# A two-layer decoder trunk on one core: order of the first contraction, place of the gates' projection, a lookup that yields, and products grouped by shape

## The chip, the cores and the metric

The kernel runs on one core of a Trainium2 chip. The metric is the device time of one execution in microseconds (us), the median of several. PE is TensorE (matmuls), DVE VectorE, ACT ScalarE, POOL GpSimd, SP the engine whose queue issues most transfers.

## What is computed

512 tokens of width 1024 go through two layers. Each layer has a mixer and a PEER channel mixer (product-key experts), each followed by a layer norm of alpha * h + sublayer(h). Cut to what matters here:

```python
def mixer_ab(x, w_in, pool_w, pool_scale, ret_norm_g, w_out):      # layer 0
    u, q, k, v, g = jnp.split(x @ w_in, AB_SPLITS, axis=-1)
    y_a = pool_mixer(u, pool_w, pool_scale)       # causal means over 2/4/8/16, then a product per group
    q, k = rotary(q), rotary(k) * 64 ** -0.5
    o = retention(q, k, v)                        # 4 heads, chunks of 128
    y_b = head_layernorm(o, ret_norm_g) * silu(g)
    return concat([y_a, y_b]) @ w_out

def hgrn2_chunkwise(q, k, v, logf):               # layer 1: 8 heads, chunks of 32
    b = cumsum(logf)                              # within a chunk
    q_in, k_in, k_out = q * exp(b), k * exp(-b), k * exp(b_last - b)
    ...

def peer(x, w_q, sub_keys, u_tab, v_tab):
    q = (x @ w_q).reshape(T, 8, 2, 128)
    s_top, i_top = top_k(einsum(q, sub_keys), 16)          # over 128 keys, per head and half
    best, pos = top_k(all sums of two halves' s_top, 16)
    eid, gate = cand_id[pos], softmax(best)                # an expert is a pair of keys
    act = gelu(einsum(x, u_tab[eid]))
    return einsum(gate * act, v_tab[eid])

h = layer_norm(alpha * h + mix);  h = layer_norm(alpha * h + peer(h))
```

All matrices are float32; u_tab and v_tab have 16384 rows of 1024.

## The kernel before

**Products.** A float32 operand is split into two fp32r parts, hi and lo: `split` lets ACT cast hi and DVE subtract to get lo (L76, L77). `mm3` then makes three matmuls per 128 rows of contraction, hi*hi, lo*hi and hi*lo (L92 to L94). `stream` loads a weight tile into `raw` over SP's queue (L82) and splits it. Nearly all weights and all experts pass this way, so ACT and DVE work for each of PE's blocks. PSUM has three pools: psA (2 tiles, pA), psB (3, pB), psC (3, pC).

**Order.** The tile scheduler keeps the order in which the program names operations on each engine as far as priorities and buffers let it. Generators (`look`, `rounds`) interleave two programs by hand: `route_topk` and `route_gates` yield a cost, and for every 2.8 of credit `lookahead` issues one block of experts (128 experts: 24 matmuls of 128x384 into one PSUM tile, then GELU into `ge`).

**Start** (`run`). The identity is loaded first, then four pairs of 256 rows of x (transposed, `xT`) and of the first weight; the pool projection then goes output by output, each over the whole contraction.

**Layer 0's mixer** (`mixer_ab`). In this order: pool projection with its sums and the product with pool_w (`pool_part`; its output times pool_scale is `ya`), gates' projection (silu into `sgs`), queries and keys with rotation, values, retention (`kn`, `sc`, `state`), normalization of the heads, output projection. `ya` is split into the output projection's operand after retention.

**Layer 1's mixer** (`mixer_c`, `decays`). For each head and each of four blocks of 128 tokens three kinds of products go to one pC tile: 128x128 (L463), two of 32x32 (L465) and one of 64x64 (L468).

**PEER** (`peer`). A layer norm per block of tokens (`tb`) writes `xT`; alpha is then multiplied into `hs` (L597). Three of the four blocks of tokens (384) go through all experts densely: `route_topk` finds keys, `lookup` turns positions into key numbers ka and kb by comparing and summing over 16 candidates on DVE (L794 to L803), PE transposes ka, kb and gate into pC (L730), and `route_gates` builds one-hot matrices `oh` (L758, against the iota `iot` of L744) and `og` (L759) and multiplies them into a dense gate matrix (L765, L766), stored as `gd`. The fourth block (tb = 3) gathers its experts' rows by indirect transfers instead. Meanwhile `lookahead` computes the first NLA groups of 4 blocks; all but the last KEEP of them are spilled to DRAM (`sp`) and come back later. `experts` then loads `gt` from `gd`, multiplies `ge` by it (L884), splits into ch and cl and accumulates the product with v_tab (L914) into six PSUM tiles, while the remaining blocks are computed.

## Time and profile before

| | us |
|---|---|
| median of three runs | 2922.81 (2922.74 to 2922.95) |
| profiled execution | 2923.92 |
| its span, first to last instruction | 2922.1 |
| PE busy | 2880.0 |
| DVE busy | 2388.3 |
| ACT busy | 1170.4 |

A busy share is a mean over stages. The stages in order of the profiled execution: layer 0's mixer to about 170 us, its routing with blocks ahead to 545, its experts to about 1410; layer 1's mixer to about 1680, routing to 2053, experts to the end.

### The profile page before, as it was taken

The page shows a single profiled execution, that of the slowest core. Times are in us where ns is not written, and L with a number is a line of the kernel's source. Part 1 is how long each engine was busy: PE and PEld are TensorE (multiplying, and loading weights), DVE is VectorE, ACT ScalarE, POOL GpSimd, SP SyncE. Part 2 cuts the span into 40 slices and gives each one's busy share as a digit, 9 for nine tenths or more (in the row PEclk, how much of TensorE's full clock was granted, in tenths as well). Part 3 has the DMA queues.
Part 4 walks back from the last instruction along what each step waited for, and adds up shares of the span by engine and source line. Part 5 has one row for each costly group of instructions (what it writes and reads, how often), then busy time and mean ns, then how long its engine had stood idle before and what let it go on. Part 6 is the DMA issues. An engine that isn't in the chain of part 4 may idle for free.

```text
span 2922.1 us, 42467 instructions
## 1 busy us (share of the span) xinstructions
PE 2880.0 (99%) x15822; PEld 2564.3 (88%) x15822; DVE 2388.3 (82%) x4500; ACT 1170.4 (40%) x1730; POOL 697.1 (24%) x538
## 2 busy tenths in 40 slices
PE   8999999999999999999999999999999999999998
PEld 6788999988888888888888889999988898898897
DVE  5679999788888888886687689999788888888875
ACT  3233555433333333334433433655433333333333
POOL 0000000144444444440000000000344444444420
PEclk9999999999999999999999999999999999999999
DMA  6232469999999989994322233489999999999972
GB/s 219 80 105 98 134 207 296 317 372 337 351 329 347 355 332 339 359 337 161 99 80 69 87 102 113 145 255 291 361 346 336 353 339 340 351 345 336 359 283 69
DMA packets 282927, 740.26 MB, mean 253 GB/s; under 512 B 21600, under 2 KB 120416, under 8 KB 282720
## 3 DMA queue, kind: packets, MB, share of 16 engines
q1 hardware_dynamic: 208992, 469.08, 46.3%
q0 software_dynamic: 73728, 268.47, 24.7%
q8 instruction: 124, 2.03, 0.3%
q14 instruction: 83, 0.68, 0.1%
HBM read 667.73 MB, written 69.73 MB: 252 GB/s over the span
## 4 chain that ended last, share of the span: by engine, by line
PE 87%; DVE 10%; issue 1%; ACT 1%; DMA 1%; POOL 0%; SPq 0%; ACTq 0%; POOLq 0%; DVEq 0%
PE pC L914 18%; PE pB L914 18%; PE pA L92 15%; PE pA L93 15%; PE pA L94 15%; PE pB L765 2%; DVE lo L77 1%; PE pB L766 1%; DVE s L677 1%; DVE ix L679 1%; DVE ix L676 1%; DVE stop L675 0%; DVE xp L795 0%; DVE xp L794 0%; DVE oh L758 0%
## 5 line engine op out<-in xcount | busy, mean ns | idle before, releaser
L77 DVE TENSOR_TENSOR lo<-raw,hi 128x1024 fp32r<-128x1024 f32 x608 | 739.9, 1219 | 190.3 <-ACT hi L76 186.5
L92 PE MATMUL pA<-xThi,hi 128*128 128x384 f32 (+2 forms) x2496 | 861.9, 345 | 12.0 <-ACT hi L76 8.7
L76 ACT CAST hi<-raw 128x1024 fp32r<-128x1024 f32 x608 | 638.3, 1052 | 587.8 <-PE pA L93 480.2
L93 PE MATMUL pA<-xTlo,hi 128*128 128x384 f32 (+2 forms) x2496 | 858.8, 344 | 0.7 <-DVE xTlo L155 0.7
L94 PE MATMUL pA<-xThi,lo 128*128 128x384 f32 (+2 forms) x2496 | 858.3, 344 | 0.0
L814 POOL DMA_INDIRECT row<-in_u,eid x256 | 390.6, 1526 | 942.4 <-DVE av L824 628.9
L92 PEld LDWEIGHTS pA<-xThi,hi 128*128 128x128 f32 x2496 | 470.3, 188 | 34.6 <-ACT hi L76 9.2
L93 PEld LDWEIGHTS pA<-xTlo,hi 128*128 128x128 f32 x2496 | 470.4, 188 | 21.8 <-DVE xTlo L155 0.9
L94 PEld LDWEIGHTS pA<-xThi,lo 128*128 128x128 f32 x2496 | 470.2, 188 | 16.2 <-DVE lo L77 0.9
L76 ACT CAST ch<-ge 128x384 fp32r<-128x384 f32 x256 | 131.7, 515 | 626.0 <-PE pC L914 493.1
L814 POOL DMA_INDIRECT row<-in_v,eid x256 | 300.1, 1172 | 179.4 <-DVE h L833 111.7
L833 DVE SCALAR_TENSOR_TENSOR h<-row,cf,h 128x1024 f32<-128x1024 f32 x256 | 328.5, 1283 | 0.0
L824 DVE CUSTOM_DVE_ANT_0 row<-row,x 128x1024 f32<-128x1024 f32 x256 | 311.5, 1218 | 0.0
L914 PE MATMUL pC<-hi,ch 128*128 128x512 f32 x768 | 300.8, 392 | 0.0
L914 PE MATMUL pB<-lo,ch 128*128 128x512 f32 x768 | 300.5, 391 | 0.0
L914 PE MATMUL pC<-hi,cl 128*128 128x512 f32 x768 | 300.0, 391 | 0.0
L914 PE MATMUL pB<-hi,cl 128*128 128x512 f32 x768 | 299.3, 390 | 0.0
L914 PE MATMUL pB<-hi,ch 128*128 128x512 f32 x768 | 298.9, 389 | 0.0
L914 PE MATMUL pC<-lo,ch 128*128 128x512 f32 x768 | 298.5, 389 | 0.0
L77 DVE TENSOR_TENSOR cl<-ge,ch 128x384 fp32r<-128x384 f32 x256 | 142.6, 557 | 178.6 <-ACT ch L76 175.5
L914 PEld LDWEIGHTS pC<-lo,ch 128*128 128x128 f32 x768 | 144.2, 188 | 32.0
L914 PEld LDWEIGHTS pB<-hi,cl 128*128 128x128 f32 x768 | 144.1, 188 | 31.8
(252 smaller groups left out, 3432.9 us busy)
## 6 DMA issues: line engine op xcount, KB each, us to landing
raw<-in_peer_ut SPq DMA_DIRECT2D x256, 512.0 KB
raw<-in_peer_v SPq DMA_DIRECT2D x256, 512.0 KB
gd<-gbuf SPq DMA_DIRECT2D x24, 2048.0 KB
gt<-gd SPq DMA_DIRECT2D x64, 768.0 KB
sp<-ge SPq DMA_DIRECT2D x22, 768.0 KB
ge<-sp SPq DMA_DIRECT2D x22, 768.0 KB
raw<-in_peer_w_q SPq DMA_DIRECT2D x32, 512.0 KB
raw<-in_c_w_in SPq DMA_DIRECT2D x32, 512.0 KB
```

The source lines that it names most:

```text
L76: self.nc.scalar.copy(hi, src)
L77: return self.nc.vector.tensor_tensor(lo, src, hi.bitcast(F32), ALU.subtract)
L92: nc.tensor.matmul(ps, ah, bh, start=(i == 0), stop=False)
L93: nc.tensor.matmul(ps, ah, bl, start=False, stop=False)
L94: nc.tensor.matmul(ps, al, bh, start=False, stop=(i == n - 1))
L676: nc.vector.max_index(out=ix[:, 0:8], in_max=mx[:, 0:8], in_values=sc)
L677: nc.vector.match_replace(out=s2, in_to_replace=mx[:, 0:8], in_values=sc, imm_value=NEG)
L765: nc.tensor.matmul(pg[:, sl], oh[:, 0, a, :, b], og[:, 0, a, :, b], start=True, stop=False)
L814: nc.gpsimd.indirect_dma_start(out=t, out_offset=None, in_=io[name], in_offset=bass.IndirectOffsetOnAxis(ap=self.eid[:, j:j + 1], axis=0))
L824: nc.vector.tensor_tensor_reduce(ur, ur, x3, 1.0, 0.0, ALU.mult, ALU.add, av[:, k:k + 1])
L833: nc.vector.scalar_tensor_tensor(acc, vr, coefs[i // GQ][:, i % GQ:i % GQ + 1], acc, ALU.mult, ALU.add)
L914: nc.tensor.matmul(acc[hf], a[:, ts], b[:, hf * 512:(hf + 1) * 512], start=first and i == 0, stop=last and i == 2)
```

## The change

- `run`: 14 matmuls on a zeroed tile are issued first (`warm`); x and the first weight come in chunks as before, but the first pair in two halves each; the identity is loaded after them.
- `proj_T` with `early="k"`: the pool projection goes over four quarters of the contraction outermost, with the four outputs in two pA and two pB tiles; `mm3` gets `first` and `last` for that.
- `mixer_ab`: the pooling sums follow the queries and keys' projection; the gates' projection follows retention, with the splits of `ya` and the transposes of the heads inside its sink; they write the old `xT`.
- `decays`: the three kinds of products are issued kind by kind for the four blocks of tokens.
- `peer`: alpha is applied to `hs` only for tb = 3 (on ACT), and for the others in the addition at the end of `experts`; the iota is made before routing.
- `lookup` yields between its steps; every second block of the look-ahead uses a pC tile; NLA is 14 instead of 13; the yield of a gate step is 1.4 instead of 1.2.

```diff
-NLA = 13
+NLA = 14
-ALT = False
-Y2 = 1.2
+Y2 = 1.4
-    def mm3(self, ps, pairs):
+    def mm3(self, ps, pairs, first=True, last=True):
...
+        if early == "k":
+            pss = [self.psA.tile([P, 512], F32, name="pA", tag="pA") for _ in range(2)] + \
+                  [self.psB.tile([P, 512], F32, name="pB", tag="pB") for _ in range(2)]
+            ops = [pairs(i, slice(0, T)) for i in range(4)]
+            for a, b in ((0, 2), (2, 4), (4, 6), (6, 8)):
+                for i in range(4):
+                    self.mm3(pss[i], ops[i][a:b], a == 0, b == NDC)
+                    if b == NDC:
+                        sink(j * 4 + i, pss[i])
+            return
...
             self.proj_T(w, 1, xT, sink_qk)
+            for n in range(4):
+                sums(n)
...
-            yT = self.new_xT()
-            for n in range(4):
-                self.split(ya[n], yT[0][:, n, :], yT[1][:, n, :])
...
+            def sink_g(j, tb, ps):
+                sg = ab.tile([P, 512], F32, name="sg%d" % tb, tag="sg%d" % tb)
+                nc.scalar.activation(sg, ps, AF.Sigmoid)
+                nc.vector.tensor_tensor(sg, sg, ps, ALU.mult)
+                nc.vector.tensor_tensor(sg, sg, ng, ALU.mult)
                 ov = o[:, tb].rearrange("p h e -> p (h e)")
-                nc.vector.tensor_tensor(ov, ov, sgs[tb], ALU.mult)
-                self.transpose_in(ov, yT, 4, 4, tb)
-        return yT
+                nc.vector.tensor_tensor(ov, ov, sg, ALU.mult)
+                if tb % 2:
+                    c = slice((tb - 1) * P, (tb + 1) * P)
+                    for n in range(4):
+                        self.split(ya[n][:, c], xT[0][:, n, c], xT[1][:, n, c])
+                if tb:
+                    turn(tb - 1)
+
+            self.proj_N(w, 3, xT, sink_g)
+            turn(NTB - 1)
+        return xT
...
                 for tb in range(NTB):
-                    t0 = tb * P
-                    ts = slice(t0, t0 + P)
+                    ts = slice(tb * P, (tb + 1) * P)
                     nc.tensor.matmul(pc[:, ts], k[:, ts], q[h][:, ts], start=True, stop=True)
+                for t0 in range(0, T, P):
                     for c in (0, 2):
                         nc.tensor.matmul(pc[32 * c:32 * c + 32, t0 + 32 * c + 32:t0 + 32 * c + 64],
...
+                for tb in range(NTB):
+                    t0 = tb * P
                     nc.tensor.matmul(pc[0:64, t0 + 64:t0 + 128], kh[:, tb].rearrange("p c s -> p (c s)"),
...
-                nc.vector.tensor_scalar(hs[tb], hs[tb], ALPHA, None, ALU.mult)
+                    nc.scalar.mul(hs[tb], hs[tb], ALPHA)
...
-                self.mm1(layer, g * NB + b, xT, ge[:, b, :], ALT and (g * NB + b) % 3 == 2)
+                self.mm1(layer, g * NB + b, xT, ge[:, b, :], b % 2 == 1)
...
-                kk = self.lookup(rs2, pos, i0, i1, thr, i16)
-                yield 9.0
+                kk = yield from self.lookup(rs2, pos, i0, i1, thr, i16)
...
             nc.vector.tensor_tensor(x, x, cst[:, None, None, :].broadcast_to(sx), op)
+            yield 2.0
             nc.vector.tensor_tensor(x, x, val[:, :, None, :].broadcast_to(sx), ALU.mult)
+            yield 2.0
...
-                    nc.vector.tensor_tensor(z, z, accs[tb][hf], ALU.add)
+                    nc.vector.scalar_tensor_tensor(z, z, ALPHA, accs[tb][hf], ALU.mult, ALU.add)
...
+    def warm(self):
+        nc = self.nc
+        with self.tc.tile_pool(name="wm", bufs=1) as wm:
+            z = wm.tile([P, 512], F16, name="z", tag="z")
+            nc.gpsimd.memset(z, 0.0)
+            ps = self.psC.tile([P, 512], F32, name="pC", tag="pC")
+            for _ in range(14):
+                nc.tensor.matmul(ps, z[:, :P], z, start=True, stop=True)
...
+            if k == 0:
+                wr = self.raw.tile([P, 2, T], F32, name="raw", tag="raw")
...
+                for a in range(2):
+                    nc.sync.dma_start(out=raw[:, a], in_=io["xT"][:, a, :])
+                    nc.sync.dma_start(out=wr[:, a], in_=wsrc[:, a])
+                for a in range(2):
+                    self.split(raw[:, a], xT[0][:, a, :], xT[1][:, a, :])
+                    self.split(wr[:, a], hi[:, a], lo[:, a])
```

Where the instructions stand. The new lines have other numbers: L76 and L77 become L75 and L76, L279 becomes L280, L295 L296, L463/L465/L468 L484/L487/L492, L758 and L759 L781 and L782, L884 L911.

DVE in layer 0's retention, between the decayed keys kn and the scores sc, before (`lo<-raw,hi` is the split of a weight tile, `xTlo<-ya` that of the pooling output):

```order
L279 TENSOR_TENSOR kn_762<-pC,kdec 128x512
L279 TENSOR_TENSOR kn_763<-pC,kdec 128x512
L77 TENSOR_TENSOR xTlo<-ya_188,xThi 128x512
L77 TENSOR_TENSOR xTlo<-ya_230,xThi 128x512
L77 TENSOR_TENSOR xTlo<-ya_275,xThi 128x512
L77 TENSOR_TENSOR xTlo<-ya_323,xThi 128x512
L77 TENSOR_TENSOR lo<-raw,hi 128x1024
L295 TENSOR_TENSOR sc_812<-pB,dmask 128x512
```

and now, from the last of the pool's outputs on:

```order
L391 TENSOR_SCALAR ya_514<-pB,psc 128x512
L76 TENSOR_TENSOR lo<-raw,hi 128x1024 x3
L280 TENSOR_TENSOR kn_649<-pC,kdec 128x512
L280 TENSOR_TENSOR kn_650<-pC,kdec 128x512
L76 TENSOR_TENSOR lo<-raw,hi 128x1024
L296 TENSOR_TENSOR sc_699<-pB,dmask 128x512
L296 TENSOR_TENSOR sc_701<-pB,dmask 128x512
```

The four splits of `ya` have left the place between kn and sc; one split of a weight stands there.

PE in layer 1's mixer, the products of one head's decays, before:

```order
L94 MATMUL pA<-xThi,lo 128x512
L463 MATMUL pC<-qs,kin 128x128
L465 MATMUL pC<-qs,kout 32x32 x2
L468 MATMUL pC<-qh,kh 64x64
L463 MATMUL pC<-qs,kin 128x128
L465 MATMUL pC<-qs,kout 32x32 x2
L468 MATMUL pC<-qh,kh 64x64
```

(the same three rows twice more follow), and now:

```order
L93 MATMUL pA<-xThi,lo 128x512
L484 MATMUL pC<-qs,kin 128x128 x4
L487 MATMUL pC<-qs,kout 32x32 x8
L492 MATMUL pC<-qh,kh 64x64 x4
L91 MATMUL pA<-xThi,hi 128x512
```

A head has three stretches of one shape instead of twelve. In one of the eight heads the stretch of 32x32 products is cut by other matmuls, one and six and one.

DVE at the handover from routing to the experts of layer 0, before, from the last gate step to the first cl:

```order
L759 TENSOR_TENSOR og<-oh,kT 128x2048
L77 TENSOR_TENSOR lo<-raw,hi 128x1024 x4
L884 TENSOR_TENSOR ge<-ge,gt 128x384 x3
L77 TENSOR_TENSOR lo<-raw,hi 128x1024
L884 TENSOR_TENSOR ge<-ge,gt 128x384 x2
L77 TENSOR_TENSOR cl<-ge,ch 128x384
```

and now:

```order
L782 TENSOR_TENSOR og<-oh,kT 128x2048
L76 TENSOR_TENSOR lo<-raw,hi 128x1024 x4
L911 TENSOR_TENSOR ge<-ge,gt 128x384 x2
L76 TENSOR_TENSOR lo<-raw,hi 128x1024
L76 TENSOR_TENSOR cl<-ge,ch 128x384
```

Two multiplications by gt stand ahead of the first cl instead of five; layer 1 has the same rows. Counted in the same way on PE: from the last gate matmul to the first product of the experts 170 matmuls of blocks stood, now 120. Before the first group of transposes L730 stood 17 blocks of the look-ahead, between the groups 5 and 6; now 19, 6 and 6. Between two gate steps and the next two 21 matmuls of blocks stood, now 24. In layer 0, eight transposes of the layer norm follow eight others without a block of the projection between them, as they already did in layer 1. On SP's queue two loads of v_tab stand between the last store of gd and the first load of gt, before and now.

## Rows read from the trace of the kernel before

**Rows 1.** The page: busy time of each engine, the chain that ended last by engine, and the groups of split operations (busy us, mean ns of one, idle before it).

```profile
PE 2880.0 (99%) x15822; PEld 2564.3 (88%) x15822; DVE 2388.3 (82%) x4500; ACT 1170.4 (40%) x1730; POOL 697.1 (24%) x538
...
PE 87%; DVE 10%; issue 1%; ACT 1%; DMA 1%; POOL 0%; SPq 0%; ACTq 0%; POOLq 0%; DVEq 0%
...
L77 DVE TENSOR_TENSOR lo<-raw,hi 128x1024 fp32r<-128x1024 f32 x608 | 739.9, 1219 | 190.3 <-ACT hi L76 186.5
...
L76 ACT CAST hi<-raw 128x1024 fp32r<-128x1024 f32 x608 | 638.3, 1052 | 587.8 <-PE pA L93 480.2
```

**Rows 2.** Windows: the stretch, its length, busy us and records of PE, PEld, DVE, ACT and POOL, then PE's granted clock, DMA share and GB/s. In order: retention's scores, the stretch behind them, the heads' normalization, the lookups of layer 0, its experts.

```profile
109.00:112.00 3.00, 2.17 (x9) 1.98 (x10) 3.00 (x6) 0.00 (x0) 0.00 (x0) 0.70 0.58 179
112.00:114.00 2.00, 2.00 (x7) 0.97 (x7) 0.35 (x2) 0.05 (x1) 0.00 (x0) 0.60 0.01 2
120.00:140.00 20.00, 19.30 (x112) 15.77 (x111) 15.81 (x51) 5.11 (x8) 0.15 (x1) 1.00 0.01 1
327.00:357.00 30.00, 26.79 (x152) 25.81 (x150) 30.00 (x124) 19.07 (x23) 0.00 (x0) 1.00 0.35 123
600.00:1400.00 800.00, 800.00 (x3916) 711.73 (x3916) 643.22 (x829) 293.13 (x407) 324.64 (x240) 1.00 0.87 323
```

**Rows 3.** Waits of PE over the whole execution: what waited and for whom, us in total, times, longest.

```profile
PE pC L730 <- DVE ka L803: 4.6, 2, 2.3
PE pC L730 <- DVE kb L803: 2.9, 4, 0.7
PE pB L765 <- DVE og L759: 2.9, 2, 1.5
...
PE pA L92 <- ACT ge L627: 1.9, 2, 0.9
```

**Rows 4.** Timeline of PE at the start: start us, us, engine, line, operation, and in brackets the idle time before and its releaser. Distances between starts count here, as ends are modelled.

```profile
8.69 0.79 PE L92 MATMUL pA<-xThi,hi 128*128 128x512 f32 x1 [8.69 <-ACT hi L76]
...
13.97 0.63 PE L94 MATMUL pA<-xThi,lo 128*128 128x512 f32 x1
14.40 0.49 PE L93 MATMUL pA<-xTlo,hi 128*128 128x512 f32 x1
...
15.20 0.39 PE L93 MATMUL pA<-xTlo,hi 128*128 128x512 f32 x1
15.42 0.39 PE L92 MATMUL pA<-xThi,hi 128*128 128x512 f32 x1
```

**Rows 5.** A memset on POOL in layer 1's mixer: duration in ns (min/median/max) and start.

```profile
L404 POOL MEMSET pb<- x1: 740/740/740, 1417.5 to 1417.5; 128x768 f32 x1
```

**Rows 6.** Timelines around retention: DVE, PE and ACT.

```profile
105.45 2.49 DVE L77 TENSOR_TENSOR xTlo<-ya,xThi 128x512 fp32r<-128x512 f32 x4
...
108.99 1.28 DVE L295 TENSOR_TENSOR sc<-pB,dmask 128x512 f32<-128x512 f32 x2
...
109.72 1.60 PE L306 MATMUL pB<-v,sc 128*128 128x128 f32 x5 [1.63 <-DVE sc L295]
...
126.93 1.28 ACT L335 ACT_TABLE_LOAD   x1
```

**Rows 7.** Timeline of PE in layer 1's decays, one block of tokens and the start of the next, and a group of eight 128x128 records of layer 0. A float32 product has two records.

```profile
1499.16 0.49 PE L463 MATMUL pC<-qs,kin 128*128 128x128 f32 x2
1499.58 0.26 PE L465 MATMUL pC<-qs,kout 128*32 128x32 f32 x4
...
1500.03 0.49 PE L463 MATMUL pC<-qs,kin 128*128 128x128 f32 x2
...
103.19 1.04 PE L278 MATMUL pC<-c_ident,r 128*128 128x128 f32 x8
```

**Rows 8.** Timeline of PE at the first transposes of a lookup, layer 0.

```profile
356.83 0.33 PE L730 MATMUL pC<-c_ident,ka 128*128 128x128 f32 x1 [2.28 <-DVE ka L803]
357.89 0.33 PE L730 MATMUL pC<-c_ident,kb 128*128 128x128 f32 x1 [0.73 <-DVE kb L803]
```

**Rows 9.** Timeline of DVE at the first gate step, layer 0.

```profile
409.89 2.36 DVE L758 TENSOR_TENSOR oh<-iot,kT 128x2048 f16<-128x2048 f16 x2 [1.76 <-POOL iot L744]
```

**Rows 10.** Timelines between layer norm and routing: PE in layer 0, PE and DVE in layer 1.

```profile
174.91 0.51 PE L92 MATMUL pA<-xThi,hi 128*128 128x256 f32 x2 [1.43 <-ACT xThi L154]
...
1681.48 0.66 PE L149 MATMUL pC<-c_ident,h 128*128 128x128 f32 x4 [1.14 <-DVE xTlo L155]
...
1681.94 0.68 DVE L597 TENSOR_SCALAR h<-h 128x1024 f32<-128x1024 f32 x1
```

**Rows 11.** Timelines at the handover from the gates to the experts: PE, DVE and ACT in layer 0, then PE and ACT in layer 1.

```profile
545.03 0.22 PE L766 MATMUL pB<-og,oh 128*128 128x128 f16 x1
...
565.16 1.50 DVE L884 TENSOR_TENSOR ge<-ge,gt 128x384 f32<-128x384 f32 x3 [4.85 <-DMA gt<-gd]
...
568.33 0.51 ACT L76 CAST ch<-ge 128x384 fp32r<-128x384 f32 x1 [4.74 <-issue]
...
573.57 0.33 PE L92 MATMUL pA<-xThi,hi 128*128 128x384 f32 x1
...
574.61 0.39 PE L914 MATMUL pB<-hi,ch 128*128 128x512 f32 x1
...
2053.48 0.22 PE L766 MATMUL pB<-og,oh 128*128 128x128 f16 x1
...
2075.24 0.51 ACT L76 CAST ch<-ge 128x384 fp32r<-128x384 f32 x1 [3.20 <-issue]
```

More of the change, by code (lines that the diff above doesn't have):

```diff
@@ L91, in mm3 @@
         for i, ((ah, al), (bh, bl)) in enumerate(pairs):
-            nc.tensor.matmul(ps, ah, bh, start=(i == 0), stop=False)
+            nc.tensor.matmul(ps, ah, bh, start=(first and i == 0), stop=False)
             nc.tensor.matmul(ps, ah, bl, start=False, stop=False)
-            nc.tensor.matmul(ps, al, bh, start=False, stop=(i == n - 1))
+            nc.tensor.matmul(ps, al, bh, start=False, stop=(last and i == n - 1))
     def wchunk(self, src, j):
@@ L218, in mixer_ab @@
             ya = []
-            self.pool_part(ab, xT, ya, w, icnt, pw, psc)
+            sums = self.pool_part(ab, xT, ya, w, icnt, pw, psc)
             nc.sync.dma_start(out=ng, in_=io["ret_norm_g"][0][None, :].broadcast_to([P, 512]))
@@ L225, in mixer_ab @@
                 nc.sync.dma_start(out=hs[tb], in_=io["x"][tb * P:(tb + 1) * P, :])
-            sgs = []
-            def sink_g(j, tb, ps):
-                sg = ab.tile([P, 512], F32, name="sg%d" % tb, tag="sg%d" % tb)
-                nc.scalar.activation(sg, ps, AF.Sigmoid)
-                nc.vector.tensor_tensor(sg, sg, ps, ALU.mult)
-                nc.vector.tensor_tensor(sg, sg, ng, ALU.mult)
-                sgs.append(sg)
-            self.proj_N(w, 3, xT, sink_g)
             qk = [None] * 4
@@ L344, in mixer_ab, with turn, sums @@
                                             ALU.subtract, ALU.mult)
-                ov = o[:, tb].rearrange("p h e -> p (h e)")
-                nc.vector.tensor_tensor(ov, ov, sgs[tb], ALU.mult)
-                self.transpose_in(ov, yT, 4, 4, tb)
-        return yT
+            def turn(tb):
+                self.transpose_in(o[:, tb].rearrange("p h e -> p (h e)"), xT, 4, 4, tb)
+            def sink_g(j, tb, ps):
[3 more added lines that the diff above has]
+                nc.vector.tensor_tensor(sg, sg, ng, ALU.mult)
+                ov = o[:, tb].rearrange("p h e -> p (h e)")
+                nc.vector.tensor_tensor(ov, ov, sg, ALU.mult)
[8 more added lines that the diff above has]
+        return xT
     def pool_part(self, ab, xT, ya, w, icnt, pw, psc):
         nc = self.nc
+        us = []
         def sink_u(n, ps):
-            u = ab.tile([P, 16 + T], F32, name="u", tag="t0")
+            u = ab.tile([P, 16 + T], F32, name="u%d" % n, tag="u%d" % n)
             nc.vector.memset(u[:, :16], 0.0)
             nc.scalar.copy(u[:, 16:], ps)
+            us.append(u)
+        def sums(n):
+            u = us[n]
             s, sh = u, 1
@@ L371, in sink_u @@
             ya.append(y)
-        self.proj_T(w, 0, xT, sink_u)
+        self.proj_T(w, 0, xT, sink_u, early="k")
+        return sums
     def mixer_c(self, xT, hs):
@@ L601, in peer @@
                 kT = rk.tile([P, TD // GW, 4, GW], F16, name="kT", tag="kT")
+                iot = rk.tile([P, P, 2], F16, name="iot", tag="iot")
+                nc.gpsimd.iota(iot, pattern=[[1, P], [0, 2]], base=0, channel_multiplier=0,
+                               allow_small_or_imprecise_dtypes=True)
                 credit = CREDIT0
-                for gen in (self.route_topk(layer, xT, kT), self.route_gates(layer, kT, gd)):
+                for gen in (self.route_topk(layer, xT, kT), self.route_gates(layer, kT, iot, gd)):
                     for cost in gen:
@@ L736, in route_topk, with route_gates @@
                 nc.vector.tensor_tensor(glT, gs, ghT, ALU.subtract)
-    def route_gates(self, layer, kT, gd):
+    def route_gates(self, layer, kT, iot, gd):
         nc, tc = self.nc, self.tc
@@ L742, in route_gates @@
         with tc.tile_pool(name="rg", bufs=2) as rg:
-            iot = rg.tile([P, P, L], F16, name="iot", tag="iot", bufs=1)
-            nc.gpsimd.iota(iot, pattern=[[1, P], [0, L]], base=0, channel_multiplier=0,
-                           allow_small_or_imprecise_dtypes=True)
             b5 = [P, 2, Q, P, L]
@@ L804, in lookup @@
             res.append(k)
+            yield 1.0
         return res
@@ L923, in run @@
         xT = self.new_xT()
+        self.warm()
         w0 = []
@@ L926, in run @@
             raw = self.raw.tile([P, 2, T], F32, name="raw", tag="raw")
+            if k == 0:
+                wr = self.raw.tile([P, 2, T], F32, name="raw", tag="raw")
+                hi = self.st.tile([P, 2, T], F32R, name="hi", tag="hi")
+                lo = self.st.tile([P, 2, T], F32R, name="lo", tag="lo")
+                wsrc = io["ab_w_in"][0, 0].rearrange("p (a n) -> p a n", a=2)
+                for a in range(2):
[4 more added lines that the diff above has]
+                    self.split(wr[:, a], hi[:, a], lo[:, a])
+                flat = "p a n -> p (a n)"
+                w0.append((hi.rearrange(flat), lo.rearrange(flat)))
+                continue
             ks = slice(2 * k, 2 * k + 2)
```

3 lines of the change are left out of this document (2 added, 1 removed).

## The prediction

> **What bounds the kernel now.** I read the page first. PE is busy 2880.0 us, 99% of the span, and the chain that ended last is 87% PE and 10% DVE [rows 1]. So only time in which PE stands still or runs slowly can be won, some tens of microseconds in all, and it has to be found stage by stage. The windows say where not to look: over 800 us of the experts stage PE is busy for every one of them at full granted clock, while around 327 to 357 us, where the keys are chosen and looked up, PE is busy 26.79 of 30 and DVE all 30 [rows 2]. There DVE decides. The waits of PE name the releasers: the lookup's products ka and kb 7.5 us over six waits, og 2.9, and the activation of a finished block, ge, 1.9 [rows 3]. Then I read PE in order of time where the change touches it: start, retention, decays, layer norm, handover to the experts.
>
> The profiled execution took 2923.92 us, 1.8 beyond its span and 1.1 above the median of the three runs, 2922.81. I sum against the former and take 1.1 off at the end. Differences under 0.2% (5.8 us) I take as what a measurement cannot tell from none.
>
> **Start.** PE begins at 8.69 us and waits until then for the first weight's hi; up to 14.40 its 14 matmuls come 0.43 apart, afterwards 0.22 to 0.23 [rows 4]. Lost now: 8.69 + 14 × 0.20 = 11.5, the few tenths around the pool's products left aside. Afterwards 14 matmuls on a zeroed tile stand ahead. The tile needs one POOL memset; the nearest row, of 768 columns, takes 0.74 [rows 5], so PE starts near 1.1. At the slow spacing 14 × 0.43 = 6.0 ends at 7.1. Halved first loads, with the identity's load behind them, should bring the first real operands before then: two loads of 512 KB take 3.2 us at 323 GB/s [rows 2] and two casts 2.1 [rows 1], half of each gives 2.6 sooner, 6.1. And with the contraction outermost four PSUM tiles share each chunk, so 24 matmuls, 5.3 us, stand behind each quarter of the contraction. Gain 11.5 − 7.1 = **4.4**. If the zero products leave the clock low, 2.8 of cold time comes back: 2 remains. If the clock rises during them, PE could start real work when the data come, at 6.1: at most 5.4.
> The Trainium skill ("TensorE: Matmul & The Clock Gate", Part 1) says that the number of cold matmuls of one kernel is not fixed: 6, 11 or 14, by the phase in which it starts. By it the profiled 14 may be a bad draw: with 6 the loss would be 1.6 smaller and so would the gain. The row shows 14, and three runs lie within 0.21 us of each other, which speaks against such a scatter here.
>
> **Retention.** DVE makes four splits of the pooling output (2.49 us) after kn, then one weight split, then sc, and PE waits 1.63 for sc [rows 6]. After this its granted clock is 0.70 in 109 to 112 and 0.60 in 112 to 114 [rows 2], that is 0.9 + 0.8 us lost. The new order has only one split of a weight between kn and sc, so sc comes 2.5 earlier, more than the wait. Gain 1.6 + 1.7 = **3.3**; 0 if DVE falls behind instead. It could: the pooling sums (18 operations on 128x512, by the splits' 0.62 each 11.2 us) now lie under the values' projection, together with four weight splits of 1.22 [rows 1]. That is 16 us of DVE under 96 matmuls × 0.22 = 21 us of PE, so it fits. The pool's own products among them wait for sums that are late only if DVE is over 5 us behind.
> The gates' projection moves behind retention and covers the heads' normalization; PE now stands still 0.70 of 20 us there [rows 2]: gain **0.5**, 0 to 0.7. It brings one more activation table load, 1.28 us [rows 6], on an ACT that is busy 5.11 of 20 us [rows 2]: hidden.
> The Trainium skill ("ScalarE: Activation LUTs", Rules for kernel authors) budgets about 2.7 us for each switch of table set and so speaks against the move. The row here has less than half of that; even 2.7 lies within ACT's idle time.
>
> **Decays of layer 1.** One block of a head runs 128x128, 2 × 32x32, 64x64 and takes 1499.16 to 1500.03, 0.87 us; the first pair takes 0.42 although the same shape back to back needs some 0.11 per record (8 in 1.04, the last one's tail included) [rows 7]. By columns the own time is 0.22 + 0.11 + 0.11 = 0.44, which leaves 0.43 for three switches of shape. Grouped, a head has 3 switches instead of 12: over 8 heads 24 blocks' switches fall away, 24 × 0.43 = 10.3. If only the switch that the row shows cleanly (0.42 − 0.22) is real: 24 × 0.20 = 4.8. I take **8.7**, nearer the columns' account, with something off as one head is still interleaved.
>
> **Routing, both layers.** The first products of the lookup wait 2.28 and 0.73 [rows 8], with DVE full; the yields inside the lookup put blocks there. Now 19, 6 and 6 blocks stand before and between the three groups of transposes, before 17, 5 and 6. A block gives PE 24 × 0.173 = 4.2 us of work (573.57 to 574.61 six matmuls [rows 11]) and costs DVE one split, 1.2 [rows 1]. So DVE gains about 6 us on the first wait and 3 on the second, against 2.3 and under 1: these waits go (7.5 in two layers). The waits on ge (1.9) come of two pA buffers for consecutive blocks; alternating with pC gives five. The comparison oh waits 1.76 for an iota on POOL [rows 9], and og behind it holds PE (2.9); the iota is made early now. Sum 7.5 + 1.9 + 2.9 = 12.3 less 0.3 for two more changes of shape among the gates: **12.0**. If ka and kb stay as they are: 4.8.
> The new yields also put 24 instead of 21 block matmuls under each two gate steps, 0.5 us more of PE beside the same work of DVE, so og gives no new wait there. Four more blocks are done ahead, and as many fewer in the experts stage, which loses nothing either way [rows 2]. They cost one more spilled group, 768 KB out and back, some 2.4 us each at that stage's 323 GB/s, under its 0.87 share [rows 2].
>
> **Layer norm to routing.** PE waits 1.43 in layer 0 and 1.14 in layer 1 [rows 10]. Three multiplies by alpha (0.68) leave DVE, the fourth goes to ACT; at the end the addition carries alpha at the same price. But in layer 0 eight transposes now follow eight without a projection between, as in layer 1 now: the fourth pC tile has to be free. I take +1.5 there and −0.6 in layer 1: loss **0.9**, between a gain of 1 and a loss of 3.
>
> **Handover to the experts.** The experts' first products need the gates through DRAM: after the last gate matmul (545.03) the store, the load of gt, DVE's multiply (which waited 4.85 for that load), then ch at 568.33, 23.3 us later, plus 1.1 for ch and cl themselves; in layer 1 2053.48 to 2075.24, 21.8 [rows 11]. PE has 170 block matmuls meanwhile, 29.4 us, and starts the first expert product at 574.61, so 5.0 and 6.5 us are spare. Now 120 are left, 20.8 us. The chain, unchanged, is 24.4 and 22.9 long; two multiplies by gt stand ahead of cl where five stood, three of 0.5 each fewer (565.16: three in 1.50). Short by 2.1 and 0.6, together 2.7, and a little low clock behind it: loss **3.0**, between 0 and 9 (with as much low clock behind as retention shows, and a slower load).
>
> **Sum.** 4.4 + 3.3 + 0.5 + 8.7 + 12.0 − 0.9 − 3.0 = 25.0. 2923.9 − 25.0 = 2898.9, less 1.1: **2897.8 us**.
>
> **Rivals.**
> (a) The forecast: every removed wait stays removed. 2898.
> (b) DVE stays the bound of routing. For it: DVE is busy all of 327 to 357, and a removed wait only lets PE ask earlier. Against it: the counts of blocks. ka and kb remain, 7.5 less: 2905.
> (c) A change of shape costs little and the long first pair is something else, say the arrival of kin. For it: the row shows no releaser, so grouping may only shift it. Against: it recurs in every block. Decays 0: 2906.
> (d) The start is bound by the data: chunks arrive no faster, and warm PE waits for them. For it: the releaser of the 8.69 is ACT's cast, which itself follows a load. Against: 24 matmuls behind each pair of chunks. With gain 0 to 2: 2901.
> (e) Other side: the handover. At 20.8 us of cover each microsecond by which gt lands later costs one per layer. To end 0.2% slower the other 28 and 5.8 more must be eaten, 17 per layer, so gt would have to land some 15 us later than now. For it: DMA is 0.87 busy, another group is spilled, and value loads stand ahead of gt in the same queue. Against: it needs three times the whole wait of today. Time then 2929.
> (b) and (c) together: 2914.
>
> **How the numbers follow.** (a) 0.60, (b) 0.12, (c) 0.08, (d) 0.10, (b) with (c) or a half-sized handover stall 0.06, (e) 0.04. The range for (a) alone: the start up to 1.0 better, decays up to 1.6 better, retention and gates 3 worse, handover 6 worse or 3 better, layer norm 2 either way: 2890 to 2907. From below I go to 2887, all the upper ends but one; above to 2910, which takes in (b), (c) and (d). Faster 0.91, within 0.2% 0.05 (2917 to 2929, several of these at once), slower 0.04.
>
> **What would show it.** Start: the first real matmul near 7 us and 0.22 apart at once. Retention: no wait for sc, granted clock 1.0 in that stretch. Decays: one stretch of 4, 8 and 4 products per head, some 1.1 us shorter. Routing: no waits of PE on ka, kb, ge, og beyond a few tenths. Handover: a new wait of PE on ch of the first expert, 1 to 3 us in each layer, or more if I am wrong. The prediction fails most easily if that wait is over 5 us, or if ka is still named in PE's waits.

## Result, and the profile after

The changed kernel takes 2893.48 us (median of four runs, 2892.6 to 2893.71) against 2922.88 (2922.74 to 2924.76): ratio 0.9897, 95% interval 0.9880 to 0.9915. 29.4 us were won where the prediction had 25.0 on the same footing (2922.8 to 2897.8). The range held the time, but the terms of the sum did not come out one by one: by the traces the start's was 5.1 too high and the others together 10.5 too low (table below), so part of the closeness is luck.

The page after, the busy times and the chain that ended last; it answers [rows 1]:

```profile
PE 2867.7 (99%) x15836; PEld 2560.2 (89%) x15836; DVE 2383.8 (82%) x4498; ACT 1169.0 (40%) x1739; POOL 708.3 (24%) x539
...
PE 93%; DVE 5%; DMA 1%; issue 1%; ACT 1%; SPq 0%; ACTq 0%; DVEq 0%
```

PE's share of the chain rose from 87 to 93%, DVE's halved, and DMA is in it with 1%, about as much as before; where it stands now is the first finding below. PE's waits after, which answer [rows 3] (what waited and for whom, us in total, times, longest):

```profile
PE pA L91 <- ACT hi L75: 2.6, 1, 2.6
PE pC L158 <- DVE xTlo L164: 2.3, 2, 1.1
PE pC L951 <- POOL z L948: 1.3, 1, 1.3
PE pA L93 <- DVE lo L76: 0.8, 2, 0.5
PE pA L91 <- ACT xThi L163: 0.7, 1, 0.7
```

ka, kb, ge, og and sc are gone from the list. A wait for hi of 2.6 us is there, and it isn't the one at the start of the kernel.

To put the 30.3 us of span (2922.1 to 2891.9) in their places I took from both traces the starts of the same PE instructions and subtracted. The gates' projection, 96 matmuls of 0.227 (21.8 us), moved from the first stretch to the third, and 146 block matmuls of 0.173 (25.3 us) are now done ahead of the last gate matmul in each layer; both are taken out of the differences.

| stretch, by PE's starts | before | after | won | forecast |
|---|---|---|---|---|
| start to the keys' transposes | 103.19 | 82.13 | −0.7 | 4.4 |
| retention, to its last state product | 22.83 | 19.30 | 3.5 | 3.3 |
| to the first routing matmul, layer 0 (gates, heads, output projection) | 48.89 | 69.46 | 1.2 | 0.5 |
| queries of routing, layer 0 | 80.09 | 79.92 | 0.2 | (with the next) |
| layer norm to the first block, layer 1 | 84.54 | 82.89 | 1.7 | −0.9, both layers |
| lookups and gates, layer 0 and layer 1 | 290.03, 290.07 | 308.66, 308.66 | 6.7 and 6.7 | 12.0 |
| last gate to the experts' first product, less the 50 matmuls moved | 29.58, 29.58 | 20.91, 20.91 | 0 | −3.0 |
| layer 1's mixer to the output transposes | 207.74 | 196.62 | 11.1 | 8.7 |
| experts (96 block matmuls fewer, 16.6 each) | 826.37, 826.37 | 809.47, 809.47 | 0.6 | 0 |
| tail behind the last product | 12.71 | 13.30 | −0.6 | 0 |

Retention after, on DVE and PE, answers [rows 6]: only one weight split (84.40) stands ahead of sc, and PE has no wait.

```profile
84.40 1.22 DVE L76 TENSOR_TENSOR lo<-raw,hi 128x1024 fp32r<-128x1024 f32 x1
85.82 1.29 DVE L296 TENSOR_TENSOR sc<-pB,dmask 128x512 f32<-128x512 f32 x2 [0.20 <-PE pC L293]
...
86.88 1.37 PE L307 MATMUL pB<-v,sc 128*128 128x128 f32 x8
```

The bracket turned round: DVE now waits 0.20 for PE. A head's decays answer [rows 7]; four blocks of tokens take 1490.29 to 1492.26, 1.97 us, where one took 0.87:

```profile
1490.29 1.06 PE L484 MATMUL pC<-qs,kin 128*128 128x128 f32 x8
1491.28 0.45 PE L487 MATMUL pC<-qs,kout 128*32 128x32 f32 x16
1491.66 0.68 PE L492 MATMUL pC<-qh,kh 128*64 128x64 f32 x8
1492.26 0.50 PE L93 MATMUL pA<-xThi,lo 128*128 128x512 f32 x1
```

The start is the place that went wrong. PE and then SP's queue (for SP the line tells when an instruction was issued):

```profile
1.32 5.94 PE L951 MATMUL pC<-z 128*128 128x512 f16 x14 [1.32 <-POOL z L948]
6.92 0.58 PE L91 MATMUL pA<-xThi,hi 128*128 128x512 f32 x1
...
29.27 0.39 PE L93 MATMUL pB<-xThi,lo 128*128 128x512 f32 x1
32.26 0.50 PE L91 MATMUL pA<-xThi,hi 128*128 128x512 f32 x1 [2.60 <-ACT hi L75]
...
33.52 0.50 PE L93 MATMUL pA<-xThi,lo 128*128 128x512 f32 x1 [0.53 <-DVE lo L76]
...
20.48 4.05 SPq L234 DMA_DIRECT2D h<-in_x  x4
24.64 30.51 SPq L81 DMA_DIRECT2D raw<-in_ab_w_in  x12
```

The first real product comes at 6.92 instead of 8.69 and finds the clock up, and the pool's last matmul is at 29.27. Then PE stands still: the next projection's first weight was issued only at 24.64, behind eight tables and four loads of h of 512 KB each. The window behind it (its length, busy us and records of PE, PEld, DVE, ACT and POOL, granted clock, DMA share, GB/s) shows the second price, a clock of 0.72:

```profile
32.00:38.00 6.00, 5.21 (x15) 3.83 (x16) 5.55 (x5) 4.89 (x6) 0.00 (x0) 0.72 0.93 311
```

At the handover, layer 0, nothing waits; the rows answer [rows 11] (PE, SP, DVE, ACT, DVE, PE):

```profile
559.48 0.22 PE L789 MATMUL pB<-og,oh 128*128 128x128 f16 x1
...
571.30 0.80 SPq L897 DMA_DIRECT2D gt<-gd  x2
...
577.77 1.03 DVE L911 TENSOR_TENSOR ge<-ge,gt 128x384 f32<-128x384 f32 x2 [3.36 <-DMA gt<-gd]
...
578.40 0.94 ACT L75 CAST ch<-ge 128x384 fp32r<-128x384 f32 x2 [0.71 <-ACT ge L654]
...
579.85 0.55 DVE L76 TENSOR_TENSOR cl<-ge,ch 128x384 fp32r<-128x384 f32 x1
...
580.39 0.39 PE L941 MATMUL pB<-hi,ch 128*128 128x512 f32 x1
```

From the last gate to the end of the first cl are 20.9 us, where the same points were 24.4 apart before. Four products with ch go ahead of the first with cl (0.9 us), so some 0.9 us were to spare.

### The profile page after: what moved, and what is told of

Same layout as the page of the kernel before. It is cut to its first block, busy times and chain, and to the rows that moved or that the text cites. A ratio compares the mean times of both kernels' runs of the same rounds, so it can differ in the third digit from the quotient of the medians.

```text
span 2891.9 us, 42555 instructions
## 1 busy us (share of the span) xinstructions
PE 2867.7 (99%) x15836; PEld 2560.2 (89%) x15836; DVE 2383.8 (82%) x4498; ACT 1169.0 (40%) x1739; POOL 708.3 (24%) x539
## 4 chain that ended last, share of the span: by engine, by line
PE 93%; DVE 5%; DMA 1%; issue 1%; ACT 1%; SPq 0%; ACTq 0%; DVEq 0%
PE pC L941 18%; PE pB L941 18%; PE pA L91 14%; PE pA L93 14%; PE pA L92 14%; PE pC L91 2%; PE pC L93 2%; PE pC L92 2%; PE pB L788 1%; PE pB L789 1%; DVE lo L76 1%; DVE oh L781 1%; DVE og L782 1%; DVE s L704 1%; PE pB L693 1%
## 5 line engine op out<-in xcount | busy, mean ns | idle before, releaser
L75 ACT CAST hi<-raw 128x1024 fp32r<-128x1024 f32 (+1 forms) x609 | 638.1, 1051 | 662.3 <-PE pA L92 459.8
L76 DVE TENSOR_TENSOR lo<-raw,hi 128x1024 fp32r<-128x1024 f32 (+1 forms) x609 | 740.1, 1218 | 198.2 <-ACT hi L75 189.1
L841 POOL DMA_INDIRECT row<-in_u,eid x256 | 397.5, 1553 | 1490.1 <-DVE av L851 583.8
L91 PE MATMUL pA<-xThi,hi 128*128 128x384 f32 (+2 forms) x2032 | 701.7, 345 | 2.6 <-ACT hi L75 2.6
L93 PE MATMUL pA<-xThi,lo 128*128 128x384 f32 (+2 forms) x2032 | 701.1, 345 | 0.8 <-DVE lo L76 0.8
L92 PE MATMUL pA<-xTlo,hi 128*128 128x384 f32 (+2 forms) x2032 | 698.1, 344 | 0.1
L91 PEld LDWEIGHTS pA<-xThi,hi 128*128 128x128 f32 x2032 | 382.3, 188 | 22.8 <-ACT hi L75 3.2
L92 PEld LDWEIGHTS pA<-xTlo,hi 128*128 128x128 f32 x2032 | 382.3, 188 | 20.0 <-DVE xTlo L164 0.5
L93 PEld LDWEIGHTS pA<-xThi,lo 128*128 128x128 f32 x2032 | 381.9, 188 | 16.0 <-DVE lo L76 1.6
L75 ACT CAST ch<-ge 128x384 fp32r<-128x384 f32 x256 | 131.5, 515 | 627.1 <-PE pC L941 477.6
L76 DVE TENSOR_TENSOR cl<-ge,ch 128x384 fp32r<-128x384 f32 x256 | 142.6, 557 | 166.9 <-ACT ch L75 164.3
```

The costliest lines, as they stand in the source:

```text
L75: self.nc.scalar.copy(hi, src)
L76: return self.nc.vector.tensor_tensor(lo, src, hi.bitcast(F32), ALU.subtract)
L91: nc.tensor.matmul(ps, ah, bh, start=(first and i == 0), stop=False)
L92: nc.tensor.matmul(ps, ah, bl, start=False, stop=False)
L93: nc.tensor.matmul(ps, al, bh, start=False, stop=(last and i == n - 1))
L841: nc.gpsimd.indirect_dma_start(out=t, out_offset=None, in_=io[name], in_offset=bass.IndirectOffsetOnAxis(ap=self.eid[:, j:j + 1], axis=0))
```

## Experiments

late_h, old_start and late_nowarm have four times each. The other runs have one each; for those the stretches of their traces carry the verdict, since the times of one kernel lie up to 1.2 us apart (seven of the kernel before up to 4.5, 2920.97 to 2925.42), and what happens behind the start's stall moves the rest (last section).

**late_h: the start's loads in another order.**

```diff
-            nc.sync.dma_start(out=ng, ...)
-            for t, n in ((cos, "cos"), (sin, "sin"), (qdec, "qdec"), ..., (cdec, "cdec")):
+            for t, n in ((cos, "cos"), (sin, "sin")):
                 nc.sync.dma_start(out=t, in_=io[n])
-            for tb in range(NTB):
-                nc.sync.dma_start(out=hs[tb], ...)
...
             self.proj_T(w, 1, xT, sink_qk)
+            # qdec, dmask, bdm, kdec, cdec, ng and the four hs[tb] are loaded here
```

> The changed kernel with one edit: the loads of h, of the gates' norm weight and of retention's tables are issued behind the weights of the queries and keys instead of ahead of them. Theory (the start's gain was given back because PE, faster now, reached the query and key weights while 3 MB of tables and of h stood ahead of them on SP's queue: 2.6 us wait for hi at 29.5 us, 0.5 for lo and some 2 us at low clock behind it): the wait is gone and the time is 4 to 5.5 us below that of the changed kernel, 2888 to 2889.5. Rival (the weights are late because the DMA engines are full, not because of the order): the wait stays, within 1 us of 2893.5.

2889.36 us (2888.67 to 2889.83, four runs), 4.1 below the changed kernel, whose runs all lie above 2892; against the kernel before 0.9883, interval 0.9866 to 0.9899. SP's queue and PE at the end of the pool projection:

```profile
16.14 3.32 SPq L81 DMA_DIRECT2D raw<-in_ab_w_in  x4
...
29.94 0.39 PE L93 MATMUL pB<-xThi,lo 128*128 128x512 f32 x1
30.16 0.39 PE L91 MATMUL pA<-xThi,hi 128*128 128x512 f32 x1
```

The weights are issued from 16.14, and the next projection follows the pool's last matmul 0.22 later. The keys' transposes are reached at 77.46 instead of 82.13; of these 4.7 us 1.7 are the low clock behind the waits, the rest the two waits themselves. So the order on the queue caused the wait, although the DMA engines are full either way (share 1.0 from 26 to 38 us in this kernel, 0.93 from 32 to 38 us in the changed kernel). This version beats both kernels.

**old_start: the start of the kernel before in the changed kernel.**

```diff
-        self.warm()
-            if k == 0:
-                ...                       # the first pair in halves
-        self.ident = self.cload("ident", [P, P])     # behind the loads
+        self.ident = self.cload("ident", [P, P])     # ahead of them
-        self.proj_T(w, 0, xT, sink_u, early="k")
+        self.proj_T(w, 0, xT, sink_u)
```

> The changed kernel with the start of the kernel before: identity first, no products on zeros, no halved loads, the pool projection output by output. Theory (the new start wins about 4 us up to the end of the pool projection and loses about 5 behind it): the time is 0 to 1.5 us below the changed kernel's, 2892 to 2893.5, and PE reaches the keys' transposes at 81.0 to 82.2 us (82.13 in the changed kernel). Rival (the prediction's term holds, 4.4 us of start saved): 2897.5 to 2898.5.

2892.45 us (2892.04 to 2892.98), keys' transposes at 81.40: all four edits at the start together are worth nothing in the changed kernel, 1.0 us less than nothing. What they do is seen at the pool's end: its last matmul stands at 33.32 here and at 29.27 in the changed kernel, 4.05 sooner, and the next projection starts at 33.55 here and at 32.26 there, with the low clock still to come. The gain was real and was handed back within 8 us; 1.7 of what was handed back is that low clock, which old_start, without the wait, does not have.

**late_nowarm: late_h without the products on zeros.**

```diff
-        self.warm()
```

> The kernel late_h without the 14 products on zeros. Theory (at the start PE soon runs into the data: the second pair of chunks is split only at 13.5 us, so warm products win little): 0.3 to 1.5 us slower than late_h. Rival (the prediction's working, each of 14 cold matmuls costs 0.20): 2.8 us slower or more.

2891.07 us (2890.14 to 2891.24), 1.7 slower than late_h, a little more than my range of 0.3 to 1.5 and far from 2.8. PE at its start:

```profile
5.05 0.79 PE L91 MATMUL pA<-xThi,hi 128*128 128x512 f32 x1 [5.05 <-ACT hi L75]
...
6.07 0.63 PE L93 MATMUL pA<-xThi,lo 128*128 128x512 f32 x1
8.93 0.80 PE L91 MATMUL pA<-xThi,hi 128*128 128x512 f32 x1 [2.23 <-ACT hi L75]
```

Three slow matmuls run out of operands at 6.07, and PE waits 2.23 for the second half. Part of the cold time lies where PE would wait anyway.

**dec_apart: the decays' products block by block again.**

```diff
                     nc.tensor.matmul(pc[:, ts], k[:, ts], q[h][:, ts], start=True, stop=True)
-                for t0 in range(0, T, P):
+                    t0 = tb * P
                     for c in (0, 2):
...
-                for tb in range(NTB):
-                    t0 = tb * P
```

> The changed kernel with layer 1's decays' products in the old order, block by block. Theory (the changes of shape are the whole difference of that stage, 11.1 us): the stretch from the first projection matmul of layer 1's mixer to the transposes for its output projection is 202 to 203 us against 191.55, the time 2904 to 2905. Rival (switches as sized in the prediction, 8.7, the rest from elsewhere): 200.2 us and 2902. Rival (the shape does not matter): 191.5.

2903.87 us, one run. The stretch of the expectation takes 202.67, as in the kernel before (202.68), against 191.56; counted from a matmul 5.1 us earlier, as in the table, it is 207.73, 207.74 and 196.62. The rows have the old period of 0.87 us:

```profile
1487.66 0.49 PE L484 MATMUL pC<-qs,kin 128*128 128x128 f32 x2
1488.08 0.26 PE L487 MATMUL pC<-qs,kout 128*32 128x32 f32 x4
...
1488.53 0.49 PE L484 MATMUL pC<-qs,kin 128*128 128x128 f32 x2
```

The grouping is the whole of that stage's 11.1 us. It pays at every shape: a pair of 128x128 records takes 0.42 here and 0.25 in the grouped head (eight from 1490.29 to 1491.28), the smaller products of a block 0.45 here and 0.25 there (those of four blocks from 1491.28 to 1492.26). What in a change of shape costs the time no run here shows.

**gates_first: the gates' projection back ahead of the queries.**

```diff
+            self.proj_N(w, 3, xT, sink_g)           # sink_g without the splits and transposes
             self.proj_T(w, 1, xT, sink_qk)
...
+            yT = self.new_xT()
+            for n in range(4):
+                self.split(ya[n], yT[0][:, n, :], yT[1][:, n, :])
...
-            self.proj_N(w, 3, xT, sink_g)
```

> The changed kernel with the gates' projection back in its old place ahead of the queries, and the splits of the pooling output with it behind retention, so that DVE again has four of them between kn and sc. Theory (those splits are what held up sc, and the low clock follows from the wait): from the keys' transposes to the last state product 22.8 us as before the change, against 19.30; with 1 us more around the heads' normalization the time is 4 to 5 us above the changed kernel, 2897.5 to 2898.5. Rival (the stretch became shorter for another reason, such as the sums placed elsewhere): 19.3 to 20.5 us and at most 2895.

2899.23 us, 5.7 above the changed kernel, 0.7 beyond the expected range. Retention takes 22.98, the stretch to routing's first matmul 48.88 (70.7 with the gates' 21.8, against 69.46). DVE and PE:

```profile
105.67 2.49 DVE L76 TENSOR_TENSOR xTlo<-ya,xThi 128x512 fp32r<-128x512 f32 x4
...
109.21 1.28 DVE L306 TENSOR_TENSOR sc<-pB,dmask 128x512 f32<-128x512 f32 x2
...
109.95 1.45 PE L317 MATMUL pB<-v,sc 128*128 128x128 f32 x6 [1.64 <-DVE sc L306]
```

The pooling sums stayed in their new place here, so it is not the cause, and the rows show the four splits ahead of sc: the theory stands. 0.8 of the rest lies in layer 0's experts, 810.27 against 809.47, without a cause that I could name.

**less_cover: fewer blocks behind the last gate.**

```diff
-Y2 = 1.4
+Y2 = 1.5
```

> The changed kernel with a yield of 1.5 instead of 1.4 for a gate step: 94 instead of 120 block matmuls are left between the last gate matmul and the experts' first product, 16.3 us instead of 20.8. Theory (the chain from the last gate through DRAM to ch is about as long as the cover now, with 1.5 us to spare at most): PE waits 3 to 4.6 us in each layer, the gap is 19.4 to 21 us instead of 16.4, and the time 6 to 10 us above the changed kernel's. Rival (the chain shortens with the cover since gt's issue follows the blocks' loads on the queue): gap 16.4 to 17.4, within 2 us of the changed kernel.

2899.94 us, 6.5 above the changed kernel. PE waits:

```profile
PE pB L941 <- DVE cl L76: 2.6, 1, 2.6
...
PE pB L941 <- ACT ch L75: 2.3, 1, 2.3
```

Both layers stall. In layer 0 the gap stayed 16.48, as the rival has it, but PE stopped four products later, at cl, and the experts take 3.05 longer; in layer 1 the gap is 18.86, 2.4 over the 16.5 that are covered, and the experts lose another 1.8, with a granted clock of 0.89 from 2070 to 2085 us (1.7 lost). With 94 matmuls of cover the chain sticks out, with 120 it just doesn't. It isn't of fixed length, though: from the last gate to the end of the first cl in layer 0 it took 24.4 us before, 20.9 after and 17.3 here, so the rival has a part in it.

**no_yield: the lookup without yields.**

```diff
-                kk = yield from self.lookup(rs2, pos, i0, i1, thr, i16)
+                kk = self.lookup(rs2, pos, i0, i1, thr, i16)
+                yield 9.0
```

> The changed kernel with the lookup as it was, without yields, and one yield of 9.0 behind it. Theory (the yields took away the waits for ka and kb by putting more blocks there): those waits come back, 7 to 8 us over both layers, time 2900 to 2902. Rival (the waits went away with the second pool of accumulators): at most 2 us slower.

2917.65 us, 24.2 above the changed kernel, three times what I had expected:

```profile
PE pC L757 <- DVE ka L827: 7.6, 2, 3.8
PE pA L91 <- ACT ge L654: 6.8, 2, 3.5
...
PE pC L757 <- DVE kb L827: 2.5, 3, 1.0
```

ka and kb hold PE for 10.1, more than the 7.5 of [rows 3]; the waits on ge that lay ahead of them (1.9) are gone, and PE probably arrives sooner by that. The waits on ge here are others, at the handover. Without the yields fewer blocks are drawn early, and 214 matmuls are left behind the last gate. There one of gt's later loads comes very late: it is issued at 572.33, behind three loads of v_tab that take 10.3 us on SP's queue. DVE and ACT of layer 0, 550.11 being the last gate matmul:

```profile
581.78 1.50 DVE L908 TENSOR_TENSOR ge<-ge,gt 128x384 f32<-128x384 f32 x3 [8.35 <-DMA gt<-gd]
...
584.92 0.51 ACT L75 CAST ch<-ge 128x384 fp32r<-128x384 f32 x1 [8.62 <-DVE ge L908]
```

ACT waits 8.62 us on ch, and the GELU of the last blocks stands behind it in the same queue, so PE's blocks find no free accumulator. That names the loss: 10.1 and 6.8 of waits, and behind them, in four places, a low clock (0.91 from 340 to 360 us, 0.83 from 580 to 600, 0.83 from 1850 to 1860, 0.89 from 2080 to 2095) that costs some 8.5, together about as much as the stretches lost.

**one_pool: all blocks in the two pA tiles.**

```diff
-                self.mm1(layer, g * NB + b, xT, ge[:, b, :], b % 2 == 1)
+                self.mm1(layer, g * NB + b, xT, ge[:, b, :])
```

> The changed kernel with all blocks of the look-ahead in the two pA tiles. Theory (alternating pools took away PE's waits on GELU, 1.9 us in two waits, and nothing else): 1.5 to 2.5 us slower, 2895 to 2896, with PE waiting on ge again. Rival (it carries the lookups' gain as well): 7 us slower or more.

2908.37 us, 14.9 above: the rival. Lookups and gates take 6.0 more in each layer (314.61 and 314.66 against 308.66), the rest is at the start (+1.5, a longer low clock, last section) and in layer 1's experts (+1.1). PE's waits, then ACT and PE at the first of them:

```profile
PE pA L91 <- ACT ge L654: 9.6, 8, 1.6
...
343.34 1.88 ACT L817 CAST xp<-pf 128x2048 f16<-128x2048 f32 x1
345.24 1.28 ACT L654 ACT_TABLE_LOAD   x1
346.54 0.49 ACT L654 ACTIVATE ge<-pA 128x384 f32<-128x384 f32 x1
...
347.08 0.44 PE L91 MATMUL pA<-xThi,hi 128*128 128x384 f32 x1 [0.90 <-ACT ge L654]
```

With the yields a block's GELU stands on ACT behind a lookup's cast (1.88) and a table load back to GELU (1.28), and two accumulators can't bridge that. In the kernel before the same wait came only twice. So the yields need the second pool, and the second pool alone doesn't remove the waits for ka and kb: neither part has a price of its own.

**iota_late: the iota at the beginning of the gates' stage.**

```diff
-                iot = rk.tile([P, P, 2], F16, name="iot", tag="iot")
-                nc.gpsimd.iota(iot, ...)
...
         with tc.tile_pool(name="rg", bufs=2) as rg:
+            iot = rg.tile([P, P, L], F16, name="iot", tag="iot", bufs=1)
+            nc.gpsimd.iota(iot, ...)
```

> The changed kernel with the iota made at the beginning of the gates' stage again. Theory of the prediction (the first oh waits for it on POOL, and og behind oh holds PE): PE waits for og about 1.5 in each layer, time 2 to 3 us above the changed kernel, 2895.5 to 2896.5. Rival (DVE now reaches the first oh so late, or PE has so many blocks left, that the iota is made meanwhile): no wait of PE over 0.3, time within 1 us of 2893.5.

```profile
PE pB L788 <- DVE og L782: 2.9, 2, 1.5
```

The wait is back at its old size, [rows 3]; lookups and gates take 1.3 longer in each layer, 2.6. The time, 2895.06, is only 1.6 above, because the keys' transposes came at 80.24 in this run instead of 82.13 (no low clock there, last section); another 0.9 is lost in the two experts stages, without a cause that I could name. The theory holds by its stage.

**alpha_early: alpha on DVE behind each layer norm.**

```diff
+                nc.vector.tensor_scalar(hs[tb], hs[tb], ALPHA, None, ALU.mult)
...
-                    nc.vector.scalar_tensor_tensor(z, z, ALPHA, accs[tb][hf], ALU.mult, ALU.add)
+                    nc.vector.tensor_tensor(z, z, accs[tb][hf], ALU.add)
```

> The changed kernel with the four multiplications by alpha back on DVE behind each block's layer norm. Theory (between layer norm and routing DVE holds PE in layer 1, and the three multiplies of 0.68 that left it are the 1.65 us by which that stretch became shorter; in layer 0 the same gain was lost to the other order of transposes): layer 1's stretch from the layer norm's transposes to the first 384-column block matmul 84.3 to 84.6 us against 82.9, layer 0's 1 to 2 us longer too, time 2895 to 2897. Rival (the multiplies are hidden and the stretch is set by the order of the transposes): both stretches unchanged, 2893.5.

2894.75 us. The stretch is 83.19 in layer 1 and 80.16 in layer 0, 0.3 and 0.2 longer than after: neither my 1.5 nor nothing. Putting alpha back brings a wait of 0.67 that the changed kernel doesn't have, but what layer 1 won is something else; the windows at the same place, before, after and in this kernel:

```profile
1683.00:1688.00 5.00, 4.72 (x27) 4.72 (x28) 5.00 (x9) 0.52 (x1) 0.00 (x0) 0.66 0.19 75
```

```profile
1661.00:1666.00 5.00, 4.96 (x42) 4.76 (x41) 5.00 (x9) 1.49 (x3) 0.00 (x0) 1.00 0.14 57
```

```profile
1661.00:1666.00 5.00, 4.57 (x39) 4.57 (x40) 5.00 (x9) 1.39 (x3) 0.00 (x0) 1.00 0.20 78
```

Before, the clock fell to 0.66 there: (1 − 0.66) × 5 = 1.7 us, the whole difference. alpha_early has the same two waits ahead of it (PE waits 1.1 and then 0.7 on xTlo) and keeps its clock.

## Why the prediction was right or wrong

**Start: the term was right where I looked and wrong as a whole.** 4.4 were forecast and 4.05 arrived at the end of the pool projection (old_start beside the changed kernel; the six other kernels that begin like the changed one get there at 29.43 to 30.08, 3.2 to 3.9 sooner than old_start). The step that failed is that I stopped there. PE reaches the next projection sooner, and I did not ask when its weights land; with the old start they had 4 us more, and were issued 3.4 us sooner as well (21.22 in old_start, 24.64 in the changed kernel), and no such wait showed. Wait, wait for lo and low clock took 4.8 us back, −0.7 in all. The rule for a moved stall, to say what is late next, I had applied to DVE and not to SP's queue. Rival (d), warm PE waiting for data, was right in kind: the large wait lay further on, but those six other kernels also wait for the second half of the first pair where (d) looked, 0.8 to 2.1 us at about 9 us, and the changed kernel's own trace is the exception.

**Zero products.** The clock was up at the first real product, as said; but late_nowarm puts them at 1.7 us and not at 2.8, as part of the cold time overlaps with waiting for data.

**Retention and gates: right.** 3.5 against 3.3; gates_first brings wait and low clock back together. The gates' cover won 1.2 by the table, where at most 0.7 were allowed: 0.7 is the wait for the heads' operand (0.68 at 132.22 in the kernel before), which is gone; 0.3 belongs to the layer norm, whose wait in front of routing is 1.14 instead of 1.43; the last 0.2 has no cause that the rows name. The additional table load was hidden, as the prediction had it.

**Decays: right in kind, too small.** 24 blocks' switches at 0.43 made 10.3, and I took 8.7 for one interleaved head. 11.1 arrived, 0.46 each, so the account by columns was close and the deduction was the error; dec_apart leaves nothing of the stage to anything but the order of the products. Rival (c) is out: the pairs got shorter in the group and nothing was shifted.

**Routing: right in sum, wrong as a sum of parts.** 13.4 against 12.0. I priced yields, second pool and iota each by the wait that it removes. The iota is separable, 2.6 of 2.9. The other two are not: taking the yields away costs 24.2, taking the pool away 14.9 (13.4 without the start's 1.5). Each wait in the list of before belonged to that order of work; another order has other waits. The fourteenth group and the gate steps' yield of 1.4 were not taken back by themselves, so their part is not known. Rival (b) is out.

**Layer norm to routing: wrong sign.** I feared +1.5 in layer 0 from eight transposes behind eight. The wait is there (1.1 in each layer), but layer 0 had one of 1.43 anyway; the stretch won 0.2. Layer 1 won 1.7 from a clock that did not fall, which I had not counted; why it did not fall stays open, since alpha_early has the waits of before and kept its clock too. Putting alpha back costs 0.3 by itself.

**Handover: the forecast loss did not come.** I had the chain at 22.9 and 21.4 us after three multiplies were taken off, against a cover of 20.8; in layer 0 it was 20.9. The step that failed is the constant distance from the last gate to gt: issued at 571.30, gt let DVE start at 577.77, 6.5 us later, where 555.34 to 565.16, 9.8 us, had gone by before. I also let the first product need cl, which comes four products later. less_cover shows that it was a near thing: 26 matmuls less, and 6.5 us are lost. Rival (e) has its mechanism, cover against the landing of gt; its size did not come.

**The sums.** Three slips in them don't bear on the result: 4.4 − 2.8 leaves 1.6 and not 2; without ka and kb 4.5 of the 12.0 remain and not 4.8; and the better ends of all of (a)'s terms together reach 2890, so 2887 lies beyond them.

## What to carry to other kernels

When a stage gets faster, look at the next loads on the queue in front of it: what stands ahead of them there, and when they land against the new time of need. Loads that are used late belong behind those used next; here that won 4.1 us with the DMA engines full either way. Don't price parts of a schedule change by one wait each and add them: two edits that each move work under the other's wait have only a common price, and taking each away by itself shows it.

## What the runs showed of the hardware

- The clock after a wait isn't settled by the length of the waits. In layer 1's layer norm the kernel before had waits of 1.14 and 0.66 us and fell to 0.66 of full clock; alpha_early had waits of 1.14 and 0.67 and stayed at 1.00. Behind the start's stall it is the same: less_cover waited 1.62 for hi and 0.53 for lo and lost clock, iota_late waited 1.82 and 0.53 and lost none.
- The start isn't the same length in kernels that begin alike, and nearly all of the difference is that clock. The keys' transposes came at 80.24 (iota_late), 81.63 (less_cover), 81.77 (no_yield), 81.93 (dec_apart), 81.95 (alpha_early), 82.13 (the changed kernel) and 83.63 (one_pool), with the same instructions up to there. The windows of iota_late, less_cover and one_pool from 30 to 45 us (the granted clock is the third number from the end):

```profile
30.00:45.00 15.00, 12.65 (x55) 10.02 (x55) 8.91 (x9) 8.06 (x9) 0.00 (x0) 1.00 0.90 337
```

```profile
30.00:45.00 15.00, 12.86 (x49) 10.00 (x48) 8.56 (x8) 7.36 (x8) 0.00 (x0) 0.89 0.88 328
```

```profile
30.00:45.00 15.00, 11.80 (x39) 9.03 (x40) 8.65 (x8) 7.32 (x8) 0.00 (x0) 0.77 0.90 329
```

  A mean of 0.89 over 15 us is 1.7 us lost, 0.77 is 3.4; the other four kernels have 0.89 there too. Less that loss all seven reach the transposes between 79.9 and 80.4. So a single time of this kernel holds 0, 1.7 or 3.4 us that the edit under test did not cause, and late_h, which takes the wait away, has a clock of 1.00 in the same window.
- The cold run at the start isn't a fixed number of matmuls. In the kernel before 12 distances of 0.43 follow one of 0.59 behind the first product; in old_start, whose loads start alike, 8 do, up to 12.5 us. The Trainium skill ("TensorE: Matmul & The Clock Gate", Part 1) says that this count differs from run to run of one kernel. These two traces, of two kernels with the same start, agree with it, and my remark in the prediction that the small scatter speaks against it was wrong.
